# Expert token slots 32 instead of 64 at two positions, and another expert beside the 160-slot one

## The chip, the cores and the metric

The kernel runs on one core of one Trainium2 chip. The metric is the device time of one execution in microseconds, which is the span from the first to the last instruction plus a few microseconds around it. Three runs of the kernel before took 1519.68, 1521.48 and 1522.76 us (median 1521.48). The profiled execution took 1520.14 us with a span of 1517.9 us, so 2.24 us lie around the span.

Engine names: PE is TensorE (matmul), PEld its weight loads, DVE VectorE, ACT ScalarE, POOL GpSimd, SP SyncE, which issues the weight transfers.

## The reference

Two layers of a transformer-like backbone over 256 latent tokens of width 1024, with 256 context tokens in the first layer. Each layer mixes tokens by attention, retention and pooling; the first then has a dense SwiGLU, the second the part that this document is about, a top-2-of-8 expert SwiGLU on the 256 latent tokens. Everything is float32.

```python
def swiglu(h, w1, w3, w2):                 # w1, w3: 1024 x 2816, w2: 2816 x 1024, one set per expert
    return (silu(h @ w1) * (h @ w3)) @ w2

def moe_swiglu(h, router, w1, w3, w2):     # h: 256 x 1024
    top_vals, top_idx = top_k(h @ router, 2)
    gates = sum(one_hot(top_idx, 8) * softmax(top_vals)[..., None], axis=-2)
    return sum(gates[:, e:e+1] * swiglu(h, w1[e], w3[e], w2[e]) for e in range(8))

x = x + g2 * rms_norm(moe_swiglu(rms_norm(x, g) * (1 + sc2) + sh2, ...), norm_post_ffn)
```

Only the 512 (token, expert) pairs that the router picks need computing. With the reference's inputs the router gives expert 0 15 tokens, and the other seven, from the most loaded to the least, 154, 90, 80, 52, 50, 46 and 25.

## The kernel before

Everything up to the router is untouched by the change; the expert stage (`experts`, L1157) starts its first matmul at 804 us of the span. It works like this.

**Positions, slots and runs.** The kernel counts each expert's tokens on the chip and sorts them: position 0 is always expert 0 (its weight addresses are static, so its loads start before the router is done), positions 1 to 7 are the other experts by falling count. `SLOTS` (L33) gives how many token slots a position has. `RUNS` (L35) gives the order: each entry is a run, and the entry with two positions runs two experts interleaved, called the pair here. Before, the runs are position 0 (64 slots), 2 (128), 4 (64), the pair of 1 (160 = 128 + 32) and 6 (64), then 5 (64), 3 (128) and 7 (64).

**Weights.** Each expert has 33 loads of 1 MB on SP's queue (`wload`, L164): 22 for `up` (w1 and w3) and 11 for `down` (w2). The buffers are a ring of 13, and six more that are lent once, so 19 loads of the first expert can be under way before the stage begins. After that a load starts when the buffer of 13 loads earlier is free. Loads are issued in the order in which the matmuls use them.

**up with few slots** (L1319, matmuls at L1339). The columns 0 to 2815 of w1 and w3 come in five pieces of 512 and one of 256. The tokens are the stationary operand (128 x slots), the weights move as plain float32. With 64 slots the 128 output partitions are cut in two groups (`tile_position`): each group takes 256 of the 512 columns, so a load, which holds four 128-row blocks of a piece, is 2 x 4 = 8 matmuls of 256 columns. With 32 slots there are four groups of 128 columns: 16 matmuls of 128 columns a load. The last, 256-wide piece (2 of the 22 loads) is 16 matmuls of 128 columns a load with either. In the trace a float32 matmul is two MATMUL and two LDWEIGHTS records; so a load of a 512-piece is 16 MATMUL records with 64 slots and 32 with 32.

**down with few slots** (L1356, L1368). A load holds two 128-row blocks of w2: 4 matmuls of 512 columns with 64 slots, 8 of 256 columns with 32.

**128 slots.** The weights of such a run are first split into two float32r parts (L161 on ACT, L162 on DVE, into three half-load buffers `whl`), and a product is three matmuls (L235 to L237). The 160-slot position takes both ways: 128 slots by the split, 32 by L1339 and L1368 from the same loads.

**Side work.** While a run is in `up`, the tokens of the next are made ready: `index` (L1218, matmuls at L1223) finds the token rows, `fetch` (L1248, L1256 on POOL) gathers them from DRAM, and `gather` (L1262) transposes them on PE (L1278) and scales them on DVE and ACT. Their rows are written to DRAM once at the start of the stage (`xrows`, L1544). Position 0 does without that: its tokens are gathered by matmuls with a one-hot matrix (L1281). PE runs its instructions in program order, so a transpose that waits for its rows holds up all behind it. `act` (L1296) does the SiLU and the product of a piece and transposes the result on PE (L1306), one load behind the piece.

**The end.** The outputs of all runs but the last go to DRAM (`scatter`, L1236); these are read back during the last run and added up, and the last run's output is added by matmuls (L1397). If an expert had more tokens than slots, a branch at L1605 would run the rest through 128-slot passes.

Of the kernel before, what the change touches and what calls it, by code (L numbers as in the profile page):

```python
# [10 lines left out]
F32 = mybir.dt.float32  # L11
# [18 lines left out]

SLOTS = (64, 160, 128, 128, 64, 64, 64, 64)  # L33

RUNS = ((0,), (2,), (4,), (1, 6), (5,), (3,), (7,))  # L35
SCRATCH = 4096
RING2, RING3 = 3, 6
MA = 3
# [7 lines left out]
def shape_constants():  # L46
# [5 lines left out]
    c[:, C_I8:C_I8 + 8] = np.arange(8)  # L52
    c[:, C_CAP:C_CAP + 8] = SLOTS
    p = np.arange(128)
# [27 lines left out]
def finish(steps):  # L82
    for _ in steps:
        pass
# [12 lines left out]
class Net:  # L97
# [1059 lines left out]
    def experts(self, pool):  # L1157
# [51 lines left out]
        def places(name, base, n, rk, w, bufs):  # L1209

            P = pool.tile([128, 2, 128], F32, name=name, tag=name, bufs=bufs)
            for t in range(2):
                v.tensor_scalar(P[:, t].rearrange("p (a s) -> p a s", s=n),
                                iota[:, None, base:base + n].to_broadcast([128, 128 // n, n]), rk(t), w(t) if w else None,
                                op0=OP.is_equal, **(dict(op1=OP.mult) if w else {}))
            return P

        def index(pos, base, n):  # L1218

            P = places("P", base, n, lambda t: rankp[:, t, pos:pos + 1], None, 1)  # L1220
            p = self.at()
            for t in range(2):
                nc.tensor.matmul(p[:, :4], lhsT=P[:, t], rhs=facts[:, t, pos], start=t == 0, stop=t == 1)  # L1223
            f = pool.tile([128, 4], F32, name="found", tag="found", bufs=4)
            v.tensor_copy(f, p[:, :4])
            src = pool.tile([128, 1], I32, name="src", tag="src", bufs=3)
            v.tensor_copy(src, f[:, 0:1])
            a = 128 // n
            i = C_ROW + 2 * (32, 64, 128).index(n)
            e = pool.tile([128, 1], F32, name="empty", tag="empty", bufs=2)  # L1230
            v.tensor_scalar(e, f[:, 3:4], cst[:, i:i + 1], cst[:, i + 1:i + 2], op0=OP.mult, op1=OP.add)
            dst = pool.tile([128, 1], I32, name="dst", tag="dst", bufs=4)
            v.scalar_tensor_tensor(dst, f[:, 1:2], float(a), e, op0=OP.mult, op1=OP.subtract)
            return src, dst, f[:, 2:3]
# [22 lines left out]
            return xr, few  # L1257

        def group(n):
            return pool.tile([128, 4, 8 * n], F32, name="few", tag=f"few{n}", bufs=1 + n // 64)  # L1260

        def gather(base, n, rk=None, w=None, got=None):  # L1262

            xr, few = got or (None, None)
            if xr is None:
                P = places("P", base, n, rk, w, 1)
            if n < 128:
                few = few or group(n)
                xs = few[:, 0].rearrange("p (k s) -> p k s", s=n)
            else:  # L1270
                xh = pool.tile([128, KB, 128], F32R, name="xh", tag="xh", bufs=1)
                xl = pool.tile([128, KB, 128], F32R, name="xl", tag="xl", bufs=1)
            for q in range(2):
                p = self.at()
                for k in range(4):
                    d = (4 * q + k) * 128
                    if xr is not None:
                        nc.tensor.transpose(p[:, k * 128:k * 128 + n], xr[:, d:d + 128], self.ident[:n, :n])  # L1278
                        continue
                    for t in range(2):  # L1280
                        nc.tensor.matmul(p[:, k * 128:k * 128 + n], lhsT=res[t][:, d:d + 128], rhs=P[:, t, :n],  # L1281
                                         start=t == 0, stop=t == 1)
                xg = xs[:, 4 * q:4 * q + 4] if n < 128 else pool.tile([128, 4, 128], F32, name="xg", tag="xg", bufs=1)
                for k in range(4):
                    kk = 4 * q + k
                    a, b = A[:, 0, kk:kk + 1], B[:, 0, kk:kk + 1]
                    if q:
                        nc.scalar.activation(xg[:, k, :n], p[:, k * 128:k * 128 + n], AF.Identity, scale=a, bias=b)
                    else:
                        v.tensor_scalar(xg[:, k, :n], p[:, k * 128:k * 128 + n], a, b, op0=OP.mult, op1=OP.add)  # L1290
                s = slice(4 * q, 4 * q + 4)
                if n == 128:
                    self.split(xh[:, s], xl[:, s], xg)
            return (xh, xl) if n == 128 else (xs, few)
# [82 lines left out]
        def adder(base, n, rk, gt_, last=False):  # L1377

            p = self.at()
            G = places("G", base, n, rk, None, 1)  # L1380
            for t in range(2):
                nc.tensor.transpose(p[:, t * 128:(t + 1) * 128], G[:, t], self.ident)
            for t in range(2):
                nc.tensor.matmul(p[:, 256:257], lhsT=G[:, t], rhs=gt_(t), start=t == 0, stop=t == 1)
            GT = pool.tile([128, 256], F32R, name="GT", tag="GT", bufs=1)
            nc.scalar.activation(GT, p[:, :256], AF.Copy)
            gcol = pool.tile([128, 1], F32, name="gcol", tag="gcol", bufs=2)
            v.tensor_copy(gcol, p[:, 256:257])
            sums = []
            if last:  # L1390

                sums = [self.at() for _ in pieces]
                for o, a in zip(sums, pieces):
                    nc.tensor.matmul(o, lhsT=self.ident, rhs=a, start=True, stop=False)
            return n, GT, gcol, sums
# [28 lines left out]
        def ready(pos, t):  # L1424


            ns = [min(128, SLOTS[pos] - b) for b in range(0, SLOTS[pos], 128)]
            t[pos] = ns, [], []
            due = []
            for i, n in enumerate(ns):  # L1430
                if pos:
                    at = index(pos, 128 * i, n)
                    t[pos][2].append(at[1:])
                    due.append((n, fetch(n, at[0])))
                else:
                    t[pos][1].append(gather(0, n, lambda t: before[:, t, 0:1], first_w))
                yield
            for n, got in due:
                t[pos][1].append(gather(0, n, got=got))

        def last_gate():
            g = pool.tile([128, D], F32, name="fgate", tag="xh", bufs=1)
            s = self.gscr[1, 1, 0]
            nc.gpsimd.dma_start(g, bass.AP(tensor=s.tensor, offset=s.offset, ap=[[0, 128], [1, D]]))
            return g
# [15 lines left out]
        def add_up():  # L1461

            accs = pool.tile([128, 2, D], F32, name="macc", tag="sums", bufs=1)
            pieces.extend(accs[:, t, c:c + 512] for t in range(2) for c in (0, 512))
            more = pool.tile([128, 2, D], F32, name="more", tag="acts", bufs=MA)
            for i, a in enumerate((accs, more)):
                nc.gpsimd.dma_start(a, self.found[SEQ * i:SEQ * i + SEQ].rearrange("(t p) d -> p t d", p=128))
            yield
            yield
            with self.behind(self.latest(DVE)):  # L1470
                for t in range(2):
                    v.tensor_add(accs[:, t], accs[:, t], more[:, t])

        def last_sums():
            pos, = RUNS[-1]
            return adder(0, SLOTS[pos], lambda t: rankp[:, t, pos:pos + 1], lambda t: gatep[:, t, pos:pos + 1], True)

# [78 lines left out]

        for i, run in enumerate(RUNS):
            if i == 1:
                n_over = nc.values_load(overi[0:1, NE:NE + 1], min_val=0, max_val=SEQ)
            if i == len(RUNS) - 1:  # L1560
                fgate = last_gate()
            ups, w2s = [], []
            for pos in run:
                ns, xs, _ = cur[pos]
# [7 lines left out]
            nxt = {}  # L1572
            side = chain(*(ready(pos, nxt) for pos in RUNS[i + 1])) if i + 1 < len(RUNS) else add_up()

            hold = self.behind([] if i else routed)
            for c, aTs in enumerate(zip(*ups)):
# [3 lines left out]
                else:  # L1580
                    hold.close()
                    if i == 0:
                        cur[0][2].append(index(0, 0, SLOTS[0])[1:])
            finish(side)
            last = i == len(RUNS) - 1
            if last:
# [173 lines left out]
```

## Time and profile before

| | us |
|---|---|
| three runs | 1519.68, 1521.48, 1522.76 |
| profiled execution | 1520.14 |
| its span | 1517.9 |
| expert stage, first matmul of an expert to the last | 804 to 1502 |
| PE busy in the span | 1452.5 (96%) |
| DVE, ACT busy | 823.6 (54%), 616.4 (41%) |
| data moved | 410.82 MB, 271 GB/s over the span |

Read it stage by stage: the expert stage is 698 of the 1518 us, and the change is in that stage alone. The mean clock of PE over the span is 0.985 of full speed.

### The profile page before, as it was taken

How to read it: one execution, taken by the hardware profiler on the slowest of the kernel's cores; microseconds unless marked ns; L12 is line 12 of the kernel's file. 1: busy time of each engine (PE TensorE's matmuls, PEld its weight loads, DVE VectorE, ACT ScalarE, POOL GpSimd, SP SyncE). 2: the span in 40 equal slices, each digit the busy share in tenths (PEclk: the TensorE clock that was granted, in tenths of full speed). 3: DMA queues.
4: the chain of work that ended last, by engine and by line, in shares of the span. 5: the costliest groups of instructions: out<-in, count | busy, mean ns of one | idle time of the engine just before them, and what ended most of it. 6: DMA issues, size and time to landing. Idle time of an engine off the chain costs nothing.

```text
span 1517.9 us, 22725 instructions
## 1 busy us (share of the span) xinstructions
PE 1452.5 (96%) x9006; PEld 1053.9 (69%) x9007; DVE 823.6 (54%) x1551; ACT 616.4 (41%) x983; POOL 62.5 (4%) x93
## 2 busy tenths in 40 slices
PE   7999999999999999999998999999999998999996
PEld 5677667988878888788665477764666655477762
DVE  3496687774554545778763088622454341078612
ACT  4336654423222222456641177522343331177511
POOL 1010200000000001000000010000000001010000
PEclk9999999999999999999999999999999999999998
DMA  8773223344453525353379899999998899999994
GB/s 340 278 285 146 86 98 123 141 170 163 142 206 135 207 100 186 119 186 111 118 293 420 351 416 368 370 403 419 419 355 329 326 363 393 420 421 409 409 420 180
DMA packets 62995, 410.82 MB, mean 271 GB/s; under 512 B 9428, under 2 KB 10136, under 8 KB 15648
## 3 DMA queue, kind: packets, MB, share of 16 engines
q1 hardware_dynamic: 54864, 392.19, 66.1%
q0 software_dynamic: 5616, 16.29, 2.9%
q8 instruction: 73, 1.20, 0.3%
q10 hardware_dynamic: 2400, 0.79, 0.2%
q14 instruction: 42, 0.34, 0.1%
HBM read 402.27 MB, written 6.98 MB: 270 GB/s over the span
## 4 chain that ended last, share of the span: by engine, by line
PE 84%; DVE 6%; DMA 5%; ACT 3%; issue 2%; ACTq 0%; POOL 0%; DVEq 0%; POOLq 0%
PE mm L1339 12%; PE mm L236 11%; PE mm L235 11%; PE mm L237 11%; PE mm L1368 7%; PE at L235 7%; PE at L236 7%; PE at L237 6%; PE md L373 1%; PE at L747 1%; DVE whl L162 1%; DMA more<-yrows 1%; DMA xr<-xrows,src 1%; PE at L724 1%; DMA few<-xrows,src 1%
## 5 line engine op out<-in xcount | busy, mean ns | idle before, releaser
L162 DVE TENSOR_TENSOR whl<-w,whl 128x1024 fp32r<-128x1024 f32 x310 | 374.5, 1223 | 267.6 <-ACT whl L161 259.2
L161 ACT ACTIVATE whl<-w 128x1024 fp32r<-128x1024 f32 x310 | 323.7, 1058 | 294.0 <-PE at L237 174.1
L1339 PE MATMUL mm<-w,few 128*64 128x256 f32 (+2 forms) x2528 | 225.8, 347 | 0.0
L1339 PEld LDWEIGHTS mm<-w,few 128*64 128x64 f32 (+1 forms) x2528 | 147.6, 133 | 68.6 <-issue 17.7
L1368 PE MATMUL mm<-w,few 128*64 128x512 f32 (+1 forms) x616 | 111.2, 536 | 0.0
L235 PE MATMUL mm<-hh,whl 128*128 128x512 f32 (+1 forms) x256 | 95.7, 374 | 1.2 <-ACT hh L161 1.2
L236 PE MATMUL mm<-hl,whl 128*128 128x512 f32 (+1 forms) x256 | 95.9, 375 | 0.0
L237 PE MATMUL mm<-hh,whl 128*128 128x512 f32 (+1 forms) x256 | 95.5, 373 | 0.0
L1368 PEld LDWEIGHTS mm<-w,few 128*64 128x64 f32 (+1 forms) x616 | 35.0, 129 | 70.6 <-issue 68.3
L237 PE MATMUL mm<-whl,hl 128*128 128x256 f32 (+1 forms) x240 | 80.9, 342 | 0.0
L236 PE MATMUL mm<-whl,hh 128*128 128x256 f32 (+1 forms) x224 | 75.3, 338 | 1.8 <-DVE whl L162 1.8
L1303 DVE TENSOR_TENSOR mg<-mg,mm 128x256 f32<-128x256 f32 (+2 forms) x36 | 13.6, 378 | 114.2 <-ACT mg L1302 114.2
L235 PE MATMUL mm<-whl,hh 128*128 128x256 f32 (+1 forms) x224 | 74.8, 338 | 0.0
L236 PE MATMUL at<-hl,whl 128*128 128x512 f32 (+1 forms) x192 | 71.3, 371 | 0.0
L237 PE MATMUL at<-hh,whl 128*128 128x512 f32 (+1 forms) x192 | 71.3, 371 | 0.0
L235 PE MATMUL at<-hh,whl 128*128 128x512 f32 (+1 forms) x192 | 71.2, 371 | 0.0
L367 DVE SCALAR_TENSOR_TENSOR wsum<-w,sc,wsum 128x1024 f32<-128x1024 f32 x48 | 59.7, 1281 | 20.8 <-DMA w<-in_w_mod_dram 20.8
L1302 ACT ACTIVATE mg<-mm 128x256 f32<-128x256 f32 (+3 forms) x54 | 22.8, 422 | 117.7 <-PE mm L1339 113.1
L235 PE MATMUL mm<-whl,xh 128*128 128x512 f32 (+1 forms) x144 | 57.9, 402 | 7.5 <-ACT whl L161 7.5
L236 PE MATMUL mm<-whl,xh 128*128 128x512 f32 (+1 forms) x144 | 57.2, 397 | 2.8 <-DVE whl L162 2.8
L235 PEld LDWEIGHTS mm<-hh,whl 128*128 128x128 f32 x256 | 48.2, 188 | 11.3 <-issue 2.1
L237 PE MATMUL mm<-whl,xl 128*128 128x512 f32 (+1 forms) x144 | 55.6, 386 | 0.0
(492 smaller groups left out, 2604.1 us busy)
## 6 DMA issues: line engine op xcount, KB each, us to landing
w<-in_moe_w_dram SPq DMA_DIRECT2D x258, 1024.0 KB, 11.5
w<-in_w_mod_dram SPq DMA_DIRECT2D x48, 1024.0 KB, 6.0
w<-in_ffn_w_dram SPq DMA_DIRECT2D x33, 1024.0 KB, 4.9
w<-in_w_in_dram SPq DMA_DIRECT2D x16, 1024.0 KB, 4.9
w<-in_w_out_dram SPq DMA_DIRECT2D x8, 1024.0 KB, 5.5
wa<-in_moe_w_dram SPq DMA_DIRECT2D x3, 1024.0 KB, 9.7
gate<-gscr POOLq DMA_DIRECT2D x5, 512.0 KB, 4.8
band<-in_band_dram SPq DMA_DIRECT2D x4, 512.0 KB, 7.8
```

The lines of the kernel that those rows point to most:

```text
L161: self.nc.scalar.activation(hi, x, AF.Copy)
L162: self.nc.vector.tensor_sub(lo, x, hi.bitcast(F32))
L235: mm(out, lhsT=a[0], rhs=b[0], start=start, stop=False)
L236: mm(out, lhsT=a[0], rhs=b[1], start=False, stop=False)
L237: mm(out, lhsT=a[1], rhs=b[0], start=False, stop=stop)
L367: nc.vector.scalar_tensor_tensor(x, y, c, x, op0=OP.mult, op1=OP.add)
L373: nc.tensor.matmul(p[32 * j:32 * j + 32], lhsT=self.sc[:, k], rhs=w[:, 0, j * 512:(j + 1) * 512], start=k == split, stop=k == KB - 1 and n ...
L724: nc.tensor.matmul(sp[:, :n], lhsT=qT[:, h, t * 128:t * 128 + 128], rhs=kT[:, kv, j, c0:], start=j == 0, stop=j == 1)
L747: nc.tensor.matmul(op[64 * i:64 * i + 64, side * 256:side * 256 + 256], lhsT=vt[:, b + 2 * side, kv * 64:kv * 64 + 64], rhs=src[:, b], sta ...
L1302: nc.scalar.activation(s1[:r, :c], h1[:r, :c], AF.Silu)
L1339: nc.tensor.matmul(h[i][m * j:m * j + m, :c], lhsT=x[0][:, k], rhs=t[:, k - k0, j * c:j * c + c], start=k == 0, stop=k == KB - 1, tile_pos ...
L1368: nc.tensor.matmul(y[0][m * q:m * q + m, :c], lhsT=x[0][:, b], rhs=w[:, j, c * q:c * q + c], start=f + j == 0, stop=f + j == FB - 1, tile_ ...
```

## The change

Two positions get 32 slots instead of 64: 0 (expert 0) and 7 (the least loaded). The pair becomes positions 1 and 7, and position 6 (still 64 slots) runs last. The tiles of 32 slots (`few32`) get two buffers instead of one. The scratch tile `xg` of the 128-slot gather loses its own buffer and shares the two of `mg`, the scratch of `act`.

```diff
-SLOTS = (64, 160, 128, 128, 64, 64, 64, 64)
+SLOTS = (32, 160, 128, 128, 64, 64, 64, 32)
 
-RUNS = ((0,), (2,), (4,), (1, 6), (5,), (3,), (7,))
+RUNS = ((0,), (2,), (4,), (1, 7), (5,), (3,), (6,))
...
         def group(n):
-            return pool.tile([128, 4, 8 * n], F32, name="few", tag=f"few{n}", bufs=1 + n // 64)
+            return pool.tile([128, 4, 8 * n], F32, name="few", tag=f"few{n}", bufs=2)
...
-                xg = xs[:, 4 * q:4 * q + 4] if n < 128 else pool.tile([128, 4, 128], F32, name="xg", tag="xg", bufs=1)
+                xg = xs[:, 4 * q:4 * q + 4] if n < 128 else pool.tile([128, 4, 128], F32, name="xg", tag="mg", bufs=2)
```

PE in the first run, from the first expert matmul to the transposes of the next run's tokens (`xr`); `w` is a weight buffer, `few` holds the tokens, a row with a count is that many instructions. Before:

```order
L1339 MATMUL mm<-w,few 64x256 x32
L1223 MATMUL at<-facts,P 128x4 x2
L1339 MATMUL mm<-w,few 64x256 x11
L1306 MATMUL at<-cst,mg 128x128 x2
L1339 MATMUL mm<-w,few 64x256 x21
L1223 MATMUL at<-facts,P 128x4 x2
L1339 MATMUL mm<-w,few 64x256 x8
L1306 MATMUL at<-cst,mg 128x128 x2
L1339 MATMUL mm<-w,few 64x256 x24
L1278 MATMUL at<-cst,xr 128x128 x8
```

Now:

```order
L1339 MATMUL mm<-w,few 32x128 x92
L1223 MATMUL at<-facts,P 128x4 x2
L1339 MATMUL mm<-w,few 32x128
L1306 MATMUL at<-cst,mg 128x128
L1339 MATMUL mm<-w,few 32x128 x35
L1223 MATMUL at<-facts,P 128x4 x2
L1339 MATMUL mm<-w,few 32x128 x16
L1306 MATMUL at<-cst,mg 128x128
L1339 MATMUL mm<-w,few 32x128 x48
L1278 MATMUL at<-cst,xr 128x128 x8
```

The transposes at L1278 stand behind the same 12 loads: 96 matmuls of 256 columns before, 192 of 128 columns now.

PE inside the pair's run, where the last load of the 160-slot expert's piece meets the four loads of the other expert's. Before:

```order
L237 MATMUL at<-whl,xl 128x512
L1339 MATMUL mm<-w,few 32x128 x16
L1339 MATMUL mm<-w,few 64x256 x8
L1306 MATMUL at<-cst,mg 128x128 x2
L1339 MATMUL mm<-w,few 64x256 x24
L1223 MATMUL at<-facts,P 128x4 x2
L235 MATMUL mm<-whl,xh 128x512
```

Now:

```order
L237 MATMUL at<-whl,xl 128x512
L1339 MATMUL mm<-w,few 32x128 x32
L1306 MATMUL at<-cst,mg 128x128
L1339 MATMUL mm<-w,few 32x128 x48
L1223 MATMUL at<-facts,P 128x4 x2
L235 MATMUL mm<-whl,xh 128x512
L1339 MATMUL mm<-w,few 32x128 x13
```

The other expert's four loads were 8 + 24 matmuls with 64 slots and two transposes; now the 16 of the 160-slot expert's own 32 slots and the other's 64 follow one another with one transpose between. The pair's first piece has all 80 without it.

POOL, the fetches for the pair while position 4 runs (`xr` is a `whl` buffer, `few` a 64-slot tile, `yrows` a scatter). Before:

```order
L1256 DMA few<-xrows,src 64x1024
L1245 DMA yrows<-yr,dst 640x1024
L1256 DMA xr<-xrows,src 128x1024
L1256 DMA xr<-xrows,src 32x1024
L1256 DMA few<-xrows,src 64x1024
```

Now:

```order
L1256 DMA few<-xrows,src 64x1024
L1245 DMA yrows<-yr,dst 640x1024
L1256 DMA xr<-xrows,src 128x1024
L1256 DMA xr<-xrows,src 32x1024 x2
L1245 DMA yrows<-few,dst 1280x512
```

The third fetch has 32 rows instead of 64, and goes to a `whl` buffer, of which there are three.

## Rows read from the trace of the kernel before

**Rows 1.** The page, busy time of the engines over the span

```profile
PE 1452.5 (96%) x9006; PEld 1053.9 (69%) x9007; DVE 823.6 (54%) x1551; ACT 616.4 (41%) x983; POOL 62.5 (4%) x93
```

**Rows 2.** Busy time by window, one per run of experts, the pair's two

```profile
core 0: us, PE busy (x) PEld busy (x) DVE busy (x) ACT busy (x) POOL busy (x), PEclk, DMA share, GB/s
804.00:872.50 68.50, 64.93 (x500) 36.07 (x499) 13.05 (x69) 11.78 (x26) 1.77 (x2) 0.98 0.94 382
872.50:975.00 102.50, 99.66 (x454) 78.94 (x454) 87.30 (x88) 76.51 (x84) 4.07 (x2) 0.98 0.99 389
975.00:1045.40 70.40, 66.96 (x520) 38.43 (x519) 10.03 (x39) 9.77 (x27) 3.75 (x4) 0.98 1.00 399
1045.40:1191.30 145.90, 141.08 (x1428) 101.46 (x1426) 67.82 (x79) 59.13 (x85) 4.88 (x2) 0.99 0.94 371
1191.30:1259.00 67.70, 67.70 (x399) 33.67 (x399) 25.47 (x22) 22.66 (x24) 0.08 (x1) 1.00 0.92 347
1259.00:1329.60 70.60, 64.82 (x497) 36.04 (x493) 5.95 (x18) 7.72 (x19) 3.81 (x4) 0.95 1.01 411
1329.60:1432.60 103.00, 99.62 (x458) 78.94 (x456) 86.84 (x86) 76.47 (x84) 4.69 (x3) 0.98 1.01 416
1432.60:1502.00 69.40, 65.97 (x498) 36.17 (x497) 5.58 (x10) 5.06 (x14) 2.45 (x3) 0.98 0.89 363
```

**Rows 3.** The longest waits of PE from 804 us: total, times, longest

```profile
PE at L1278 <- DMA xr<-xrows,src: 7.9, 2, 5.1
PE mm L235 <- ACT whl L161: 7.5, 4, 2.3
```

**Rows 4.** Timeline of PE, first run: start, length, instruction, idle before

```profile
803.99 7.13 PE L1339 MATMUL mm<-w,few 128*64 128x256 f32 x64
811.04 0.61 PE L1223 MATMUL at<-facts,P 128*128 128x4 f32 x4
830.63 1.09 PE L1278 MATMUL at<-cst,xr 128*128 128x128 f32 x8 [2.86 <-DMA xr<-xrows,src]
831.65 3.63 PE L1339 MATMUL mm<-w,few 128*64 128x256 f32 x16
853.38 19.10 PE L1368 MATMUL mm<-w,few 128*64 128x512 f32 x88
```

**Rows 5.** Timeline of PE and PEld in the pair's run

```profile
1083.31 1.08 PE L1339 MATMUL mm<-w,few 128*32 128x128 f32 x32
1084.32 0.50 PE L235 MATMUL at<-whl,xh 128*128 128x512 f32 x1
...
1083.31 0.81 PEld L1339 LDWEIGHTS mm<-w,few 128*32 128x32 f32 x32 [0.37 <-DMA w<-in_moe_w_dram]
...
1212.69 1.06 PE L1368 MATMUL mm<-w,few 128*32 128x256 f32 x14
1213.68 0.50 PE L236 MATMUL mm<-whl,ma 128*128 128x512 f32 x1
```

**Rows 6.** Groups by form in the pair: busy us, mean ns, idle before

```profile
L1339 PE MATMUL mm<-w,few 128*32 128x128 f32 x704 | 29.1, 282 | 0.0
```

**Rows 7.** Lines L1544 and L1256 on POOL: ns, starts, landing

```profile
L1544 POOL DMA_DIRECT2D xrows<-xt x1: 749/749/749, 807.8 to 807.8; - x1
DMA to landing us min/median/max: 12.1/12.1/12.1
...
L1256 POOLq EVENT_SEMAPHORE  x2: 17/354/692, 819.9 to 820.0; - x2
L1256 POOL DMA_INDIRECT xr<-xrows,src x1: 1022/1022/1022, 821.5 to 821.5; - x1
DMA to landing us min/median/max: 9.1/9.1/9.1
```

**Rows 8.** Line L172, the last nine weight loads: ns, starts, landing

```profile
L172 SPq DMA_DIRECT2D w<-in_moe_w_dram x9: 332/333/333, 1454.6 to 1475.3; - x9
DMA to landing us min/median/max: 20.5/20.5/21.9
```

## The prediction

> **What bounds the kernel now.** I read the page first, then windows of one run of experts each, then PE's waits. PE is busy 96% of the span [rows 1] and in every expert run 92 to 100% of its window [rows 2], so the stage is a stream of matmuls with few holes. From 804 us on, its longest waits are 7.9 us for gathered token rows and 7.5 us for the split of weights [rows 3]; waits for a weight load are not among them. The reader is to see in the windows that the transfers are close behind all the same: the DMA share is 0.89 to 1.01, and 411 to 416 GB/s where it is full. So less work on PE is gained one for one only as long as the loads can come earlier too. I take 416 GB/s as the full rate; a 1 MB load (1.049 million bytes) is then 2.52 us.
>
> **The change part by part.**
>
> *One load in `up`.* With 64 slots four loads take from 803.99 to 811.04, so 1.76 us each [rows 4]. A load with 32 slots is shown in the pair, where the 160-slot expert's odd 32 slots run: 1083.31 to 1084.32, so 1.01 us [rows 5]. The saving is 0.75 us a load for the 20 loads of the 512-wide pieces; the last two loads are 16 matmuls of 128 columns either way. The dearest reading of the same work is 29.1 us for all 22 loads, 1.32 us each, with stretches in it that run beside the split matmuls [rows 6]; then the saving is 0.44 us. I take 0.75, the undisturbed case, since in the new rows of matmuls little lies between.
>
> *One load in `down`.* 64 slots: 19.10 us for 11 loads, 1.74 each [rows 4]. 32 slots: 1212.69 to 1213.68, 0.99 us, 16 records of which the trace kept 14 [rows 5]. Saving 0.75, times 11 is 8.2 us.
>
> *First run, up to the transposes.* Nothing of the 12 loads' saving survives here, apart from a rest. The transposes at L1278 wait for `xr` until 830.63 [rows 4]. These rows are gathered out of `xrows`, whose write is issued at 807.8 and lands 12.1 us later, at 819.9; POOL's gather waits for that until 819.9, then for its index from PE and DVE until 821.5, and lands 9.1 us after that [rows 7]. PE will get to L1278 near 818 (804 + 12 x 1.01, two index steps of 0.6, two transposes) and the index will be ready before 819.9, so the gather starts 1.5 us earlier and so do the transposes, at about 829.1: 1.5 us gained, and a wait of 11 us in place of 2.86. The landing can differ by a few us either way; 0 to 4 are the ends. After the old wait 16 records took 3.63 us against 1.76 undisturbed [rows 4], so that PE lost 1.9 us; I expect the same loss after the longer wait, up to 2 us more if it lasts longer.
>
> *First run, the rest.* 8 loads of 512-wide pieces behind the transposes, 8 x 0.75 = 6.0, and `down` 8.2. With the 1.5: 15.7 us.
>
> *The pair.* The 64-slot partner becomes a 32-slot one: 20 x 0.75 + 8.2 = 23.2 us. By the dear reading it would be 8.8 + 8.2 = 17.0.
>
> *The last run* stays a 64-slot run with the same loads: 0.
>
> *The smaller edits.* `xg` in the buffers of `mg` makes the 128-slot gather and `act` take turns on ACT and DVE; in the first run that falls into PE's wait, in position 4's run ACT is busy 9.77 us of 70.4 [rows 2]. I cost it at nothing; without that cover it is one wait of about 2 us. The third fetch into a third `whl` buffer is freed by its transposes before the pair's splits start: nothing. A wait becomes shorter-covered in the pair: while the partner's four loads run, ACT and DVE split ahead for the 160-slot expert; that cover falls from 7.1 to 4.1 us a piece. DVE is busy 67.82 of 145.9 us there [rows 2], so the splits fit, but the old trace already has four waits for the split, up to 2.3 us [rows 3]. I charge 2 us over the five pieces (0 to 10).
>
> *The transfers.* Each window's spare is its length times (1 - GB/s / 416) [rows 2]: first run 5.6, second 6.7, position 4 2.9, the pair 15.8 + 11.2 = 27.0, then 0.8, 0, and 8.8 in the last, of which 6.2 lie behind the last landing: 45.6 us in all. The last load is issued at 1475.3 and lands 20.5 us later, 1495.8 [rows 8]; its matmuls begin 1.74 before 1502, at 1500.3, so 4.5 us are in hand there. PE's 15.7 in the first run against 5.6 are 10 us taken from the lead of 13 buffers (33 us), two thirds of it given back in the second run; the pair's 23.2 are inside 27.0. The total, 38.9 - 4.5 = 34.4, is inside 45.6, but not by much: I charge 2 us for late loads near the end.
>
> *Sum.* 15.7 + 23.2 - 2 - 2 = 34.9 us off the profiled execution's 1520.14: 1485.2, so I say 1485. That execution is 1.3 us under the median of the three runs and inside them; the tail behind 1502 is unchanged.
>
> **The rivals.**
>
> *PE is not fed fast enough (slower).* The 1.01 us is a burst of 32 weight loads and 32 matmuls between split matmuls. The first run will ask for 384 such pairs up to L1278 and 256 behind it, with little between, the pair's run for up to 160 in a row. The fastest long stretch shown is 64 + 64 records in 7.05 us, 18 a us [rows 4]; the burst is 63 a us [rows 5]. In between no row says anything. A 32-slot load is 64 records, so the change loses in `up` if PE can be fed fewer than 36 a us (64 / 1.76). At 25 a us a load takes 2.56: L1278 would be reached near 836.5, 6 us late, 8 loads lose 6.4, the pair loses 5 x (3 x 0.8 - 0.75) = 8, the first load of each piece being a burst, and `down` at 1.28 a load gives 10 back: some 10 us slower, 1530. At 18 a us the same steps give 1575. For it: the burst follows split matmuls, behind which instructions can pile up ready to go. Against: the records inside the burst show no slowing. The Trainium skill, TensorE: Matmul & The Clock Gate, in its table of specifications, gives PE's queue as 64 deep, exactly the burst, by which the burst proves nothing about longer rows; no row here has more. The same page's section Back-to-back issue gap gives about 81 ns a matmul of 128 columns in a sustained stream of load and matmul pairs; by that, an estimate, a load is 2.6 us and the time about 1531. The burst's 32 ns a record disagrees with it over 32 records [rows 5].
>
> *The transfers bind (a smaller gain).* By the share instead of the bytes, the DMA engines are idle only 4.1 + 1.0 + 0 + 8.8 + 5.4 + 0 + 0 + 1.4 = 20.7 us before the last landing [rows 2]. If that is all that can be given back, the gain is 20.7 + 4.5 = 25 and the time 1495, with waits for `w` loads in the last runs. For it: three runs are at a share of 1.00 and more. Against: in the pair a share of 0.92 moves 347 GB/s and 1.01 moves 416, so the share flatters how full it is.
>
> *No change.* The dear reading of `up` (17.0 and 13.2), late rows in the first run (-4) and the split's 10 leave about 16; feeding near 36 a us takes the rest: 1520.
>
> *The change does not do what it says.* More than 32 tokens at position 0 or 7 would send the kernel into the branch, at least one more 128-slot pass like the second run's 102.5 us [rows 2]. The inputs give 15 and 25 tokens, so it won't.
>
> **How the numbers follow.** Forecast 0.65, its own range 1478 to 1493. A gain cut by the transfers or by feeding between 36 and 60 a us, 1493 to 1517, 0.20. No change, within 0.2% (3 us, about what a measurement of this kernel can tell from none) 0.03. PE fed too slowly 0.11, the branch 0.01: slower 0.12. So faster is 0.85. The range 1477 to 1512 leaves out the slower cases, no change, and a little at either end.
>
> **What would show it.** Right: 32-slot loads of 1.0 to 1.1 us all along the first run; one wait of about 11 us at L1278 for `xr`, ending near 829; the second run starting near 857, position 4's near 959, the pair 191 to 193 us long instead of 214 with its waits on `whl` a little up; the stage's last expert matmul near 1467; DMA at over 400 GB/s in the pair. Wrong: 32-slot matmul records whose spacing grows after the first 32 of a row (feeding); PE waiting for `w` loads by more than 5 us in sum (transfers); a second pass at L1605; or L1278 released well off 829.

## The result, and the profile after

The changed kernel takes 1478.61 us (median of four runs, 1476.22 to 1483.48) against 1521.91 before: ratio 0.9722, 95% interval 0.9695 to 0.9749. Run once more later, it gave 0.9699 (0.9677 to 0.9722). Forecast were 1485 and a range of 1477 to 1512; the time lies 1.6 us above the range's lower end. The profiled execution has a span of 1476.6 us, 41.3 less than before.

Windows of the same stretches as in [rows 2], with the new borders (first run, second run, position 4, the pair's `up` and `down`, position 5, position 3, last run):

```profile
core 0: us, PE busy (x) PEld busy (x) DVE busy (x) ACT busy (x) POOL busy (x), PEclk, DMA share, GB/s
805.80:860.60 54.80, 41.56 (x903) 33.25 (x902) 10.72 (x59) 10.45 (x26) 1.77 (x2) 0.83 0.94 377
860.60:962.30 101.70, 98.18 (x457) 77.86 (x456) 87.30 (x88) 76.34 (x84) 4.07 (x2) 1.00 1.01 415
962.30:1031.70 69.40, 66.96 (x520) 38.36 (x519) 9.88 (x39) 9.40 (x27) 3.70 (x4) 0.98 1.01 414
1031.70:1161.20 129.50, 123.66 (x1745) 96.32 (x1746) 67.45 (x80) 58.31 (x86) 1.89 (x2) 0.99 1.01 416
1161.20:1216.10 54.90, 54.90 (x485) 33.66 (x484) 25.17 (x21) 22.34 (x23) 0.00 (x0) 1.00 1.00 410
1216.10:1286.70 70.60, 64.59 (x499) 36.17 (x495) 5.74 (x18) 7.42 (x19) 3.91 (x4) 0.95 1.01 420
1286.70:1390.40 103.70, 100.83 (x458) 79.85 (x456) 86.86 (x86) 76.46 (x84) 2.46 (x3) 0.97 1.01 415
1390.40:1461.10 70.70, 65.96 (x498) 36.11 (x497) 5.57 (x10) 5.08 (x14) 2.45 (x3) 0.98 0.90 370
```

Read the lengths first: the first run 54.8 us instead of 68.5, the pair 184.4 instead of 213.6, all others within 1.3 us of what they were. Then the last two columns: from the second run to the last but one every window moves 410 to 420 GB/s, where [rows 2] had 347 to 399 in the first five. The loads now come earlier by using idle time of the weight queue, and little of it is left: by the prediction's sum (length times 1 - GB/s / 416) 9.1 us in all, 5.1 of them in the first run, where 45.6 were. Load by load it is the same: from load 20 to the last, the landings fall behind a steady 2.49 us each by 74 us in sum before, by 35 now (which includes the time that gathers and scatters take on the same engines).

PE's waits in the expert stage (line, what it waited for, total, times, longest), to be read beside [rows 3]:

```profile
PE at L1278 <- DMA xr<-xrows,src: 18.2, 3, 11.5
PE mm L235 <- ACT whl L161: 7.3, 4, 2.3
PE at L1306 <- DVE mg L1303: 7.3, 7, 4.0
...
PE mm L1339 <- issue: 1.9, 2, 1.0
```

There is no wait for `w`. The waits for splits are 7.3 us, as before (7.5). The wait of 11.5 us is the forecast's, in the first run. Its timeline (start, length, instruction, idle before), beside [rows 4]:

```profile
805.78 7.82 PE L1339 MATMUL mm<-w,few 128*32 128x128 f32 x184
...
833.26 1.97 PE L1278 MATMUL at<-cst,xr 128*128 128x128 f32 x8 [11.50 <-DMA xr<-xrows,src]
835.16 1.94 PE L1339 MATMUL mm<-w,few 128*32 128x128 f32 x32
...
839.13 2.83 PE L1339 MATMUL mm<-wa,few 128*32 128x128 f32 x96
841.89 0.33 PE L1306 MATMUL at<-cst,mg 128*128 128x128 f32 x1
...
850.90 9.70 PE L1368 MATMUL mm<-w,few 128*32 128x256 f32 x176
```

Three loads of 32 slots in a row take 2.76 us from their start to the next instruction, 0.92 each (839.13 to 841.89). The first row takes 7.82 us for not quite six loads, 1.36 each: PE's granted clock is 0.50 there until 811.2 us, the level of 1.2 GHz, and it is again in the transposes behind the wait (1.97 us against 1.09 in [rows 4]).

### The profile page after: what moved, and what is told of

It reads as the page before. It is cut to its first block, busy times and chain, and to the rows that moved or that the text cites. A ratio compares the mean times of both kernels' runs of the same rounds, so it can differ in the third digit from the quotient of the medians.

```text
span 1476.6 us, 24342 instructions
## 1 busy us (share of the span) xinstructions
PE 1400.3 (95%) x9812; PEld 1047.6 (71%) x9813; DVE 820.8 (56%) x1551; ACT 613.5 (42%) x983; POOL 57.3 (4%) x93
## 5 line engine op out<-in xcount | busy, mean ns | idle before, releaser
L1339 PE MATMUL mm<-w,few 128*32 128x128 f32 (+2 forms) x3072 | 197.9, 319 | 1.9 <-issue 1.9
L1339 PEld LDWEIGHTS mm<-w,few 128*32 128x32 f32 (+1 forms) x3072 | 140.8, 125 | 52.2 <-issue 17.4
L1368 PE MATMUL mm<-w,few 128*32 128x256 f32 (+1 forms) x792 | 89.9, 452 | 0.0
L237 PE MATMUL mm<-whl,hl 128*128 128x256 f32 (+1 forms) x240 | 79.6, 336 | 0.0
L235 PE MATMUL at<-hh,whl 128*128 128x512 f32 (+1 forms) x192 | 71.2, 371 | 0.0
L1368 PEld LDWEIGHTS mm<-w,few 128*32 128x32 f32 (+1 forms) x792 | 34.7, 119 | 51.5 <-issue 42.2
L1302 ACT ACTIVATE mg<-mm 128x128 f32<-128x128 f32 (+3 forms) x54 | 21.8, 403 | 100.9 <-PE mm L1339 95.8
L1303 DVE TENSOR_TENSOR mg<-mg,mm 128x128 f32<-128x128 f32 (+2 forms) x36 | 12.2, 339 | 89.9 <-ACT mg L1302 89.8
L235 PE MATMUL at<-whl,xh 128*128 128x512 f32 (+1 forms) x144 | 55.5, 385 | 0.0
```

Source lines behind the costliest of these rows:

```text
L235: mm(out, lhsT=a[0], rhs=b[0], start=start, stop=False)
L237: mm(out, lhsT=a[1], rhs=b[0], start=False, stop=stop)
L1302: nc.scalar.activation(s1[:r, :c], h1[:r, :c], AF.Silu)
L1303: v.tensor_mul(s1[:r, :c], s1[:r, :c], h3[:r, :c])
L1339: nc.tensor.matmul(h[i][m * j:m * j + m, :c], lhsT=x[0][:, k], rhs=t[:, k - k0, j * c:j * c + c], start=k == 0, stop=k == KB - 1, tile_pos ...
L1368: nc.tensor.matmul(y[0][m * q:m * q + m, :c], lhsT=x[0][:, b], rhs=w[:, j, c * q:c * q + c], start=f + j == 0, stop=f + j == FB - 1, tile_ ...
```

## The experiments

Each ratio is to the kernel before, from the same chip, with its 95% interval. The code shows the lines that matter, cut from longer edits. Those of e1 and e2 are against the kernel before, and both have the change's edits of the `few` and `xg` tiles as well.

**e1: the first run alone.**

```
-SLOTS = (64, 160, 128, 128, 64, 64, 64, 64)
+SLOTS = (32, 160, 128, 128, 64, 64, 64, 64)
```

> Only expert position 0 gets 32 slots; the pair stays (1, 6) and position 7 runs last with 64 slots. The prediction's term for the first run was 15.7 us, so about 1506 us against 1521.9 of the kernel before. The trace of the changed kernel says less: its pair starts 1047.15 - 1033.40 = 13.8 us earlier, after an xr wait of 11.5 us and a stretch at the lower clock level before it, so about 1508. Rival, the transfers give part of it back later (loads behind the first run can't come earlier by as much): 1512 to 1516, with waits of PE for w loads or for splits in the runs behind.

Measured 1509.45 us, 0.9893 (0.9865 to 0.9922): 14.2 us below before in the medians, 12 to 21 by the interval, which holds the forecast's 15.7 as well as the 13.8 of the trace. PE has no wait for `w`, so nothing is given back to the queue here. Its profiled execution, one of the two slowest of six, shows less: the first run is 9.2 us shorter from the routing to its end (65.3 instead of 74.5), and the pair and the last run are 1.5 and 1.7 longer, each with 3.4 us more at half the clock.

**e2: the pair alone.**

```
+SLOTS = (64, 160, 128, 128, 64, 64, 64, 32)
+RUNS = ((0,), (2,), (4,), (1, 7), (5,), (3,), (6,))
```

> Only position 7 gets 32 slots and runs beside the 160-slot expert; position 6 runs last with 64 slots; position 0 keeps 64. Prediction's term: 23.2 us less 2 for splits, so about 1501 us. Theory from the changed kernel's trace: a 64-slot load that stands alone between split matmuls costs 1.95 us, not 1.76, and a 32-slot load in a row 0.94, not 1.01, so the pair is 29.4 us shorter: about 1492.5. Rival, transfers: the two halves draw on the same idle time of the queue; then each alone gives what PE saves, and the two gains together come to more than the 43.3 of the whole change.

Measured 1488.14 us, 0.9763 (0.9739 to 0.9787). By its trace the pair, from the end of position 4's run to its own end, lasts 184.4 us, as in the changed kernel (184.5; before 213.8): 29.4 us less, so the term of 23.2 was too small and the theory from the prices is right. The median is 35.5 lower, 6 more than that: in the profiled execution 2.3 us lie ahead of the routing, where nothing was changed (see the part on why the prediction came out as it did), and 2.0 in the other runs. The two gains add up to 14.2 + 35.5 = 49.7 against 43 to 46 for the whole; the intervals are too wide to say that the halves share anything, and in the traces the stage, from the routing's first matmul to the last of an expert, is shorter by 6.2 + 31.4 = 37.6 us in the two and by 38.7 in the whole. (e1's trace has the lower clock at the start, as the changed kernel's: see e5.)

**e3: no wait for xr in the first run.** The transposes move behind the sixth load of `down`.

```
-                    with self.behind(self.latest(PE)):
-                        next(side, None)
+                    if i or c == 1:
+                        with self.behind(self.latest(PE)):
+                            next(side, None)
...
-            finish(side)
+            if i:
+                finish(side)
...
+                if f == 5:
+                    finish(side)
```

> The changed kernel, with the transposes of the second run's token rows moved from behind the third piece of up to behind the sixth load of down, in the first run only, where xr has long landed. Theory 1, PE's path is the bound: the 11.5 us wait goes, and with it the slow stretch behind it (transposes 1.97 us against 0.71, two loads 3.54 against 1.88): 14.4 us, about 1464. Theory 2, the weight queue is the bound, since it moves 415 GB/s from the second run on and the last load lands at 1455.6 and is used at about 1459.4: at most 3.8 us, 1475 to 1478.5, and PE waits for w loads instead, in the first run's down and in the second and third run.

Measured 1475.15 us, 0.9675 (0.9651 to 0.9698); the changed kernel's own 0.9699 and 0.9722 are 3.7 and 7.2 us more. So theory 1's 14.4 us don't come. Where did they go? First, into a wait that nobody had on the list. PE in the first run:

```profile
820.83 1.06 PE L1339 MATMUL mm<-w,few 128*32 128x128 f32 x26 [0.99 <-issue]
...
827.57 1.06 PE L1339 MATMUL mm<-w,few 128*32 128x128 f32 x27 [2.46 <-issue]
...
833.45 1.07 PE L1339 MATMUL mm<-wa,few 128*32 128x128 f32 x29 [1.60 <-issue]
...
839.34 1.93 PE L1339 MATMUL mm<-w,few 128*32 128x128 f32 x30 [1.60 <-issue]
```

"issue" is a wait for nothing that the profile shows; here the tiles had landed long before. Between two of these waits stand 127 or 128 matmul records and as many weight loads, 256 instructions, and in the record of transfers one packet of 16 KB on the instruction queue starts 2.4 us before each wait ends (818.46, 825.17, 831.10, 836.95). I read this as PE running out of instructions: 6.7 us in four waits. All 24 such waits of the stage in the 13 traces, none of them in the kernel before, end 2.2 to 2.6 us after the start of such a packet; no run here changes the supply alone. Second, the clock: the first run is 7.4 us shorter than the changed kernel's (57.3 instead of 64.7 from the routing to its end), but the second is 3.1 longer, with its first 6.9 us (857.3 to 864.2) at half the clock. Third, the queue. The last loads of the last run:

```profile
1450.24 1.94 PE L1368 MATMUL mm<-w,few 128*64 128x512 f32 x8 [0.70 <-DMA w<-in_moe_w_dram]
1452.73 1.94 PE L1368 MATMUL mm<-w,few 128*64 128x512 f32 x8 [0.56 <-DMA w<-in_moe_w_dram]
1455.22 1.94 PE L1368 MATMUL mm<-w,few 128*64 128x512 f32 x8 [0.55 <-DMA w<-in_moe_w_dram]
1457.72 1.94 PE L1368 MATMUL mm<-w,few 128*64 128x512 f32 x8 [0.56 <-DMA w<-in_moe_w_dram]
```

They start 2.49 us apart, the pace at which loads land; the last run is 1.9 us longer than the changed kernel's. Such waits stand in no row of the changed kernel.

**e4: one more buffer for loads ahead.**

```
+                        [lambda: self.work.tile([128, 2048], F32, name="wf", tag="few64", bufs=2)]
```

> The changed kernel with one more buffer lent to the weight loads at the start of the stage (the second few64 buffer, which nothing uses in the first run): one load more is fetched before the queue stops at about 808. Theory 2, the queue is the bound: every later load lands one load earlier, 2.5 us; as PE's own work is close behind, 1 to 2.5 us off 1478.6, so 1476 to 1477.5. Theory 1, PE is the bound: no change, 1478 to 1479.

Measured 1478.49 us, 0.9703 (0.9679 to 0.9728): no change that can be told. Its profile had the full clock at the start (see e5) and is 3.6 us shorter than the changed kernel's; there the last load lands 0.5 us ahead of its matmuls, where the changed kernel has 3.8 us. So the queue is at PE's heels, but the time alone doesn't settle which is the bound.

**e5: the changed kernel again.**

> The changed kernel once more, as the yardstick of this set: its ratio to the kernel before was 0.9722 (0.9695 to 0.9749), so 0.970 to 0.975. Its trace tells whether the 12 us at the lower clock level at the start of the first run belong to the change (then they are here again) or come and go.

Measured 1478.10 us, 0.9699. The stretch at the lower clock is in its trace too, but it also comes without the change. The windows in which PE gathers the first expert's rows, in the changed kernel, in e4 (32 slots as well) and in e8 (64 slots, as before):

```profile
799.00:805.80 6.80, 6.80 (x36) 6.74 (x34) 2.62 (x21) 0.00 (x0) 0.00 (x0) 0.50 1.01 420
```

```profile
800.60:804.20 3.60, 3.60 (x35) 3.55 (x33) 1.69 (x15) 0.00 (x0) 0.00 (x0) 1.00 1.03 428
```

```profile
801.60:808.50 6.90, 6.90 (x35) 6.78 (x33) 3.19 (x23) 0.00 (x0) 0.00 (x0) 0.50 1.01 423
```

The column behind POOL is the granted clock. The clock falls to the 1.2 GHz level behind PE's wait of 1.5 us for the routing in some profiles and not in others, with either number of slots (of 13 traces five at full length, 10 to 14 us, three for part of it, five not at all or only later). Four of the eight traces with 32 slots at position 0 have it at full length, and one of the five with 64; whether 32 slots make it more frequent is not settled by so few. From that wait to the end of the first run it takes 64.7 us in the changed kernel and 60.7 in e4; 79.6 in e8 and 74.5 before.

**e6: e3 and e4 together.**

> Later transposes (e3) and one more buffer (e4) together. If the weight queue is the bound, what each gave stands side by side: e3 left PE waiting for w loads at the end, so one more load in hand is worth up to 2.5 us there: about 3 us below e3, ratio 0.965 to 0.966. If PE is the bound, no better than e3's 0.9675.

Measured 1474.39 us, 0.9679 (0.9654 to 0.9703): no better than e3, so the expected 3 us are not there. Its waits from 1200 us on say why nothing more comes:

```profile
PE mm L1339 <- DMA w<-in_moe_w_dram: 4.4, 6, 2.0
PE mm L1368 <- DMA w<-in_moe_w_dram: 2.9, 5, 0.7
```

**e7 and e8: PE has less to do in one place.**

```
                             for q in range(128 // m):
+                                if self.thin and 0 < f + j < FB - 1 and (j or q):
+                                    continue
...
+            self.thin = i == 2
```

> The changed kernel with 30 of the 44 matmuls left out in down of the third run (position 4): PE has 9 to 13 us less to do there, at 0.434 us a matmul (19.10 us for 44), the lower end if the lone ones that stay cost twice that; all loads stay. If the weight queue is the bound now: 0 to 4 us off (0.969 to 0.9722), with waits of PE for w loads later on. If PE is: 9 to 13 us off (0.964 to 0.966).

> The same 30 matmuls left out of the kernel before. Its queue has idle time behind this place (between 1045 and 1259 us the loads land 22 us later in sum than back to back), so by both theories PE's 9 to 13 us come off: 0.991 to 0.994. If it gives less than 5, leaving these matmuls out is worth less on PE than I think, and e7 tells nothing.

Measured 1473.09 us, 0.9681 (0.9652 to 0.9709), for the changed kernel and 1512.46 us, 0.9918 (0.9891 to 0.9945), for the one before: 5 us off the one (against 1478.10), 10 off the other. The intervals overlap in what they take off, so the times alone don't decide. The traces do: position 4's run is 6.5 us shorter in e7 and 6.9 in e8 (62.9 and 63.5 us), somewhat less than the 9 us that I took as the lower end. In e8 PE has no wait for `w` of half a microsecond behind that place; in e7 it does, 4.8 + 2.2 us from 1200 us on, and its last run takes 74.5 us where the changed kernel's takes 70.7 (in the pair ACT's split, too, waits 3.2 us for `w`, and PE 1.1 us behind it):

```profile
PE mm L1339 <- DMA w<-in_moe_w_dram: 4.8, 6, 1.3
...
PE mm L1370 <- DMA w<-in_moe_w_dram: 2.2, 4, 0.6
```

**e9 and e10: four loads less in the queue.**

```
+                if not (self.thin and f > 12):
+                    w = self.wload(w2(f), 2, D)
...
+            self.thin = i == 2
```

> The kernel of e6 with four weight loads left out: in down of the third run the last four use the tile of the load before them. PE's work is unchanged, and the queue has 4 x 2.49 = 10 us less to move. If the queue is what now ends the stage, PE's waits for w loads in the last run (6.1 us in sum in e6's trace) go: 5 to 6 us off e6, ratio 0.964 (0.962 to 0.966), and no wait for w behind the third run. If PE ends it: no change, 0.967 to 0.969.

> The same four loads left out of the kernel before, whose queue still has 48 us of idle time behind that place: by both theories no change, 0.998 to 1.001.

Measured e9 1467.74 us, 0.9643 (0.9613 to 0.9672), as expected from the queue. But e10, which should have stood still, gives 1517.19 us, 0.9957 (0.9937 to 0.9977). Fewer loads also changed the order in which the instructions were laid out. PE at the start of the pair in e10:

```profile
1049.08 1.08 PE L1339 MATMUL mm<-w,few 128*32 128x128 f32 x32
1050.09 0.50 PE L235 MATMUL mm<-whl,xh 128*128 128x512 f32 x1
```

and in the kernel before, where the odd 32 slots' row is cut in two to fill a wait for splits:

```profile
1047.15 0.50 PE L235 MATMUL mm<-whl,xh 128*128 128x512 f32 x1 [1.73 <-ACT whl L161]
1047.58 1.06 PE L1339 MATMUL mm<-w,few 128*32 128x128 f32 x26
...
1051.33 0.42 PE L1339 MATMUL mm<-w,few 128*32 128x128 f32 x6
```

32 records in two pieces take 1.06 + 0.42 us, in one 1.08. The pair of e10 is 5.8 us shorter by this, by the wait that is gone, and by 3.4 us at half the clock that only the kernel before has there. The pair of e9 is 2.8 us shorter than e6's, so about half of e9's gain of 5.5 us may be that; PE waits 2.7 us less for splits in it, of which 1.0 was, in e6, a wait of ACT for `w`. What shows of the queue is the last run, 71.2 us instead of 74.7, and no wait for `w` from 1200 us on. This control failed as a control, and that the queue gave more than those 3.5 us and that 1.0 is not shown.

**e11: the partner's loads in twos.**

```
...
+                    elif f % 2 or f == FB // 2 - 1:
+                        for _ in range(1 + f % 2):
+                            yss[k] = next(d)
```

> The kernel before, with the 64-slot partner's down loads in the pair taken two at a time behind two of the 160-slot expert's, work and loads unchanged. If what a 64-slot load costs beyond 1.74 us there (2.94 us for 24 records less 0.99 for the odd 32 slots is 1.95) is paid by the first load of a row, two in a row take 1.95 + 1.74, so rows of 32 records of about 4.7 us (with the 0.99 ahead of them) stand where 2 x 2.94 stood with one 0.99 of it apart, and the pair's down is 5 x 0.2 = 1 us shorter. If a 64-slot load beside split matmuls simply costs 1.95 wherever it stands: no shorter.

One run, 1521.49 us; the pair is 216.1 us long, 2.3 longer and not 1 shorter. In its row

```profile
1234.85 0.63 PE L1368 MATMUL mm<-w,few 128*32 128x256 f32 x4
...
1238.69 5.22 PE L1368 MATMUL mm<-w,few 128*32 128x256 f32 x40
```

the two 64-slot loads start at 1239.255 and the 32 slots behind them at 1242.839: 3.58 us, against 1.87 for one alone (1251.410 to 1253.277 in the kernel before). So 1.72 each and 0.15 once: the price is that of the change of form at either side, as I thought, though smaller. What was lost came from the odd 32 slots, now in six pieces of four records, at 0.63, and five of eight, where the kernel before had most of them in one row with a 64-slot load.

## Why the prediction came out as it did

By the steps of the sum, in the profiled executions (us gained):

| | forecast | measured |
|---|---|---|
| up to the transposes of the first run | 1.5 | -2.6 (830.6 to 833.3) |
| rest of the first run | 14.2 | 14.5 |
| second run, position 4 | 0 | 1.9 |
| the pair | 23.2 - 2 | 29.3 |
| the three runs behind it | -2 | -2.2 |
| tail | 0 | 0.4 |
| sum | 34.9 | 41.3 |

Of the 41.3 us, 2.1 are not the change's: from 48 to 54 us of the span, ahead of all that was changed, PE's granted clock was 0.55 in the profile of the kernel before and 1.00 in the other, so that the routing comes at 795.9 us instead of 798.0. In e3, e4, e6 and e9, which have the same slots, it comes at 798.0 to 798.3. Counted from the routing, the first row is -4.8 and the sum 39.2. That the forecast came so near is in part luck: by that count the pair gave 8.1 us more than its 21.2, and the front of the first run 6.3 less.

**The bound and the mechanism: right.** PE's matmuls set the time, and their savings came off nearly one for one, in the first run behind the transposes and in the pair.

**A load's saving of 0.75 us: too small, and this is the main step that made the forecast 6.4 us too long.** I took 1.76 for 64 slots from a row of such loads and 1.01 for 32 slots from a load that stands alone between split matmuls. These are unlike places: the first hardly holds the change of form, the second holds all of it. Like for like, in a row, it is 1.72 and 0.86 in `down` (groups of records, one to each column tile, 0.429 and 0.216 us apart, four groups to a load) and 1.73 and 0.87 in `up` (0.216 and 0.109 apart, eight to a load). In the pair a 64-slot load stood beside 32-slot ones and paid for the change on its own; a 32-slot load there joins the row. The kernel before in the pair, `up` and `down`:

```profile
1087.32 2.96 PE L1339 MATMUL mm<-w,few 128*32 128x128 f32 x48
1090.21 0.44 PE L1306 MATMUL at<-cst,mg 128*128 128x128 f32 x2
1090.57 5.40 PE L1339 MATMUL mm<-w,few 128*64 128x256 f32 x48
1095.90 0.27 PE L1223 MATMUL at<-facts,P 128*128 128x4 f32 x1
...
1251.41 2.94 PE L1368 MATMUL mm<-w,few 128*64 128x512 f32 x24
1254.28 0.50 PE L235 MATMUL mm<-whl,ma 128*128 128x512 f32 x1
```

and the same places in the changed kernel:

```profile
1093.46 1.96 PE L1339 MATMUL mm<-w,few 128*32 128x128 f32 x64
1095.35 0.33 PE L1306 MATMUL at<-cst,mg 128*128 128x128 f32 x1
1095.61 2.83 PE L1339 MATMUL mm<-w,few 128*32 128x128 f32 x96
1098.36 0.71 PE L1278 MATMUL at<-cst,few 64*128 64x64 f32 x8
...
1176.17 1.93 PE L1368 MATMUL mm<-w,few 128*32 128x256 f32 x32
1178.04 0.50 PE L235 MATMUL mm<-whl,ma 128*128 128x512 f32 x1
```

From start to start: a piece of `up` 2.89 + 5.33 = 8.22 us before and 1.89 + 2.75 = 4.64 now, 3.6 saved where 3.0 were forecast; a load of `down` 2.87 and 1.87, 1.00 where 0.75 was. Over five pieces and eleven loads that is 17.9 + 11.0 = 28.9 of the 29.3 measured; forecast were 23.2.

**The first run up to the transposes: wrong by its sign, right in its mechanism.** The wait was forecast as 11 us ending near 829; it was 11.5 ending at 833.26. POOL in the changed kernel, beside [rows 7]:

```profile
809.54 0.75 POOL L1544 DMA_DIRECT2D xrows<-xt  x1 [45.51 <-ACT xt L1543]
822.49 1.02 POOL L1256 DMA_INDIRECT xr<-xrows,src  x1 [12.20 <-PE mm L1339]
```

The write of `xrows` is issued 1.7 us later, 3.8 us when counted from the routing: it waits for ACT's scaled rows, which stand behind the first gather, and that ran at the lower clock. It lands at 821.56, 12.0 us on; the gather starts 0.9 us behind that, where it was 1.6 before and the forecast had none, and takes 10.7 us instead of 9.1, for which no run shows the cause. Even in e4, with the full clock there, `xr` lands 33.1 us behind the routing, 0.5 later than before. So 1.5 us expected, 0.5 to 4.8 lost, counted from the routing.

**The first run, the rest: right in size, by two errors that cancel.** From the transposes on it is 27.3 us instead of 41.9: `down` gave 9.4 instead of 8.2 by the in-row prices, and the part ahead of it 5.1 instead of 6.0, since the stretch at half the clock behind the wait (until 838.5) and a wait of 0.9 us for instructions took some back.

**The 2 us charged for splits: not paid; the 2 us for late loads: right in size, for another reason.** The waits for splits didn't grow. The three runs behind the pair are 2.2 us longer, but not by `w` loads: the last load lands at 1455.6 for matmuls that begin at 1461.1 - 1.74 = 1459.4, 3.8 us in hand against 4.5. 1.4 of it is the last run's wait for DVE at L1306, 4.05 us where it was 2.69.

**The transfers' 45.6 us of spare: right.** By the same sum some 37 of them were used, by the landings 39. The rival reading by the share (20.7 us, a gain of 25) is refuted. But the forecast missed how near the end of it lies: e3, e6 and e7 take 6 us and more off PE's path, get 3 to 7, and PE then waits for `w` in the last run.

**PE not fed fast enough: the rival lost here, but its mechanism exists.** A row of the pair in the changed kernel, and one of the last, 256-wide piece of the first run in the kernel before:

```profile
1049.46 4.58 PE L1339 MATMUL mm<-w,few 128*32 128x128 f32 x160
```

```profile
850.46 1.97 PE L1339 MATMUL mm<-w,few 128*64 128x128 f32 x32
```

The row of 160 records ran at 28.6 ns a record, 70 matmul and load records a us, so 25 a us didn't hold. It need not have been feared: the second row, with records 55 ns apart, is 37 a us, twice the 18 that the forecast took for the fastest long stretch, and two such rows with two transposes between them are 33 a us over 3.9 us. The Trainium skill (TensorE: Matmul & The Clock Gate, Back-to-back issue gap) gives about 81 ns a matmul of 128 columns in a sustained stream of load and matmul pairs; the row of 160 disagrees, by 28.6 ns a record, or 57 a matmul where each leaves two records. What the rows of the kernel before could not show is the 256th instruction: in e3, with nothing to stop PE, 128 records take 5.9 us, 43 matmul and load records a us in all, above the break-even of 36 but below the 70 of the row of 160. In the changed kernel it cost two waits, 1.9 us; I take it that the wait for `xr` gave the instructions time to come, since e3, without that wait, has 6.7 us in the same run.

**Left open.** How much of e9's gain is the queue's; and what a kernel would take whose first run neither waits for `xr` nor runs out of instructions. Why the clock falls at the start of the stage in some executions and not in others is open too. No version here that does all the work beats the changed kernel beyond doubt: e3 and e6 are 3 to 4 us below it in the median, within the intervals.

## What to carry to other kernels

Price an operation at the place in which it will stand: in a row or alone, next to its own form or another. Here one difference taken from unlike places made 0.75 us of 0.86 to 1.00, over the pair's 31 loads. And when a change takes work off the busy engine, add up what idle time the next resource has left: this change used some 37 of 46 us of the queue's, and by the waits of e3, e6 and e7 whatever comes next has to take bytes out of the queue as well.

## What the runs showed of the hardware that was not expected

- A row of small matmuls can outrun the supply of instructions: in e3 PE stood 1.0 to 2.5 us after each 256 of them (128 matmul records and 128 weight loads), each time until 2.4 us after a 16 KB instruction packet had begun. That it waited for the instructions is a reading of this.
- A change between matmuls on two 64-column tiles and on four 32-column tiles costs 0.12 to 0.17 us: the last group before it is 0.10 to 0.11 us longer than in a row, the first one behind it 0.02 to 0.05. A 64-slot load alone takes 1.87 us, 0.15 more than in a row.
- The clock at the start of the expert stage falls to half in some profiles and not in others, behind the same wait of 1.5 us, and moves the end of the first run by 4 to 5 us.
